# FFN outputs of the long sequence: accumulating DMA writes to DRAM in place of VectorE's additions in the plain groups

## The chip, the cores and the metric

The kernel runs on one NeuronCore of a Trainium2 chip as a single program. The metric is the device time of one execution in microseconds (us). Three runs of the kernel before took 3214.97, 3220.68 and 3206.7 us; their median, 3214.97 us, is the time before.

The engines are named as the profile names them: PE (TensorE matmuls; PEld is its weight load), DVE (VectorE), ACT (ScalarE), POOL (GpSimd) and SP (SyncE). DMA transfers are issued from two queues: SP's, which loads weights and inputs, and GpSimd's, which moves intermediate data to and from DRAM and is the one used for transfers that add into their destination.

## The reference

One encoder layer runs over two sequences, a sample of 1024 tokens ("s") and a prompt of 512 ("p"), D_MODEL = 1024:

```python
mod = (silu(c) @ w_ada + b_ada)                       # nine vectors of 1024 for each sequence
hn = rmsnorm(x, ffn1_norm) * (1 + sc1) + sh1
x = x + 0.5 * g1 * ((silu(hn @ w_gate) * (hn @ w_up)) @ w_down)     # FFN1, D_FF = 2816
hn = rmsnorm(x, mix_norm) * (1 + sc2) + sh2
proj = hn @ w_in                                       # q, k, v and three hyena inputs
x = x + g2 * (concat(rmsnorm(attention), rmsnorm(hyena)) @ w_out)
hn = rmsnorm(x, ffn2_norm) * (1 + sc3) + sh3
x = x + 0.5 * g3 * ((silu(hn @ w_gate) * (hn @ w_up)) @ w_down)     # FFN2
y = rmsnorm(x, final_norm)
```

The hyena branch convolves with long filters that come from a small network of the position; the filters do not depend on x, so they can be computed at any time before the mixer.

## The kernel before

Activations lie transposed, [feature, token], in 128 x 512 slices: eight slices (`KT`) for each chunk of 512 tokens, two chunks c for s and one for p. A product in fp32 is made of three matmuls on parts in fp32r: high weights by high activations, low by high, high by low. The parts of a weight (`hl<-raw`) are made by ACT and DVE, those of an activation (`act<-a`) too.

**The FFN of s** (`ffn`, L526) runs in 11 groups of two blocks of 128 hidden features. In a group, gate and up products go into PSUM tiles `gu`, ACT applies silu (`s<-gu`), DVE multiplies (`a<-s,gu`), and the parts `act` are made. Then `down` (L540) makes the group's share of the output: for each chunk eight slices dt, each of six matmuls of 512 columns into one of the two PSUM buffers of tile `dn`. That share, times the gain `Gc_s` of the layer's modulation, must be added to the residual x, which lies in SBUF as `q.xT` (tiles `xTs` in FFN1, `xRs` in FFN2; prompt: `xTp`, `xRp`).

A number `change` (7 in FFN1, 4 in FFN2) splits the groups in two sorts. Groups 0 to change-1 are plain. The later ones run in `ffn_fast` (L739), which saves matmuls by a scheme of seven products and needs more SBUF: the blocks in which x lies. The handover is in the last plain group, at L573 to L576: `spill_x` (L510) copies x to DRAM (`xscr_s`) by sixteen DMAs of 256 KB on GpSimd's queue, the side work is drained (below), and `Fast` takes x's blocks. In the plain groups before that, DVE adds each slice to x in SBUF, one instruction for each:

```python
stt(xv, ps, q.Gc[:, k, dt:dt + 1], xv, ALU.mult, ALU.add)
```

In the last plain group and in those of `ffn_fast`, `gather` (L520) does it instead: ACT scales the PSUM slice into an SBUF tile y (`pp`), and GpSimd issues a DMA that adds y to x in DRAM:

```python
se.activation(y, ps, AF.Copy, scale=q.Gc[:, k, dt:dt + 1])
nc.gpsimd.dma_start(q.xscr[c][dt], y, accum_op=ALU.add)
```

In the last group `reload_x` brings x back (tile `xRs<-xscr_s`).

**The order of the work.** A list scheduler sets each engine's order at build time; the chip keeps it. What it is given comes from `merge` (L1465), which interleaves the FFN with side work at a pace set by PLAN: the side work's progress follows that of the main work, measured in estimated engine time, against a total `mt`, 548e3 in stage A and 400e3 in stage E. ACT's and DVE's instructions of side work get a lower priority (LAG).

Stage A is FFN1 of s. Its side work is the filters of s, then a part of the modulation vectors (`ada_rest`: 1 MB loads into two buffers, `wada6a` and `wada6b`, on SP's queue, read by matmuls `mx<-wada6a,cs`), then the filters of p. For each of its eight steps a filter loads a small weight (`r<-in_hy_wo`, GpSimd's queue), splits it on ACT (`mscA<-r`) and DVE, makes the filter on PE and DVE, sums its absolute values on DVE (`r<-fT6b`), sums over channels on PE (`mx<-r,ones`), transforms it on PE and writes it to DRAM (`kscr_s`, `kscr_p`, GpSimd's queue). For p the transformed filter lies in tile `fT6b`, which the next step writes again.

Stage E is the hyena's end, the output projection and FFN2 of s. Its side work is p's mixer: attention, hyena, output projection (x of p is loaded from DRAM in halves, `xh6b<-xscr_p`, and written back), and the norm before FFN2 of p, whose parts go to DRAM (`nscr_p`).

At the start of the program the two chunks of x (`xin<-in_x_s`) are loaded, transposed on PE and copied to `xTs`, the modulation weights are loaded and multiplied, and the first FFN weights follow, all on SP's queue.

Of the kernel before, what the change touches and what calls it, by code (L numbers as in the profile page):

```python
# [11 lines left out]
F32 = mybir.dt.float32  # L12
# [5 lines left out]
P = 128  # L18
D = 1024
KT = D // P  # L20
# [72 lines left out]
def build(ctx, tc, nc, A):  # L93
# [34 lines left out]
    def mm(out, lhsT, rhs, start, stop, resume=False):  # L128
        work["pe"] += size(rhs) * (0.42 if rhs.dtype == F32R else 1.68)
        nc.tensor.matmul(out, lhsT, rhs, start=start, stop=stop, skip_group_check=resume)  # L130
# [5 lines left out]
    def tt(out, a, b, op):  # L136
        work["dve"] += 62.0 + 1.05 * size(out)
        ve.tensor_tensor(out, a, b, op=op)

    def stt(out, a, s, b, op0, op1):  # L140
        work["dve"] += 62.0 + 1.17 * size(out)
        ve.scalar_tensor_tensor(out, a, s, b, op0=op0, op1=op1)
# [8 lines left out]
    def dma(out, in_):  # L151
        nc.sync.dma_start(out, in_)

    def dmb(out, in_):
        MB.dma_start(out, in_)  # L155
# [4 lines left out]
    def gu():  # L160
        return pp.tile([P, 512], F32, tag="gu", bufs=3, name="gu")
# [9 lines left out]
    def t_s(shape=(P, 512), dt=F32):  # L171
        return fp.tile(list(shape), dt, tag="s", bufs=2, name="s")

    def t_a(shape=(P, 512), dt=F32):
        return fp.tile(list(shape), dt, tag="a", bufs=2, name="a")
# [4 lines left out]
    def t_act(shape=(P, 1024), dt=F32):  # L180
        return fp.tile(list(shape), dt, tag="act", bufs=4, name="act")

    def t_raw():
        return wp.tile([P, 1024], F32, tag="raw", bufs=3, name="raw")

    def t_hl():
        return wp.tile([P, 2, 512], F32R, tag="hl", bufs=6, name="hl")
# [13 lines left out]
    for qn, L in SEQ_LEN.items():  # L201
        q = Seq()
# [147 lines left out]
    def load_unit(src, dims):  # L350
        raw = t_raw()
        rv = raw if len(dims) == 0 else raw.rearrange("p (a b) -> p a b", b=dims[-1])
        dma(rv, src)
        hs = []
        for h in range(2):
            hl = t_hl()
            rh = raw[:, h * 512:(h + 1) * 512]
            se.activation(hl[:, 0], rh, AF.Copy)
            tt(hl[:, 1], rh, hl[:, 0].bitcast(F32), ALU.subtract)
            hs.append(hl)  # L360
        return hs

    def col_unit(w, c0):

        hs = load_unit(w[:, c0:c0 + P].rearrange("(kt p) c -> p kt c", p=P), (KT, P))
        return [[hs[kt // 4][:, i, (kt % 4) * P:(kt % 4 + 1) * P] for kt in range(KT)] for i in range(2)]

    def gemm_cols(ps, wv, xh, xl):
        gemm_along([ps], [wv], xh, xl)

    def gemm_along(pss, wvs, xh, xl, kts=range(KT)):

        for kt in kts:
            for ps, wv in zip(pss, wvs):
                mm(ps, wv[0][kt], xh[kt], kt == 0, False)
                mm(ps, wv[1][kt], xh[kt], False, False)
                mm(ps, wv[0][kt], xl[kt], False, kt == KT - 1)
# [132 lines left out]
    def spill_x(q):  # L510
        for c in range(q.C):
            for k in range(KT):
                dmb(q.xscr[c][k], q.xT[c][:, k])
# [6 lines left out]
    def gather(q, k, c, dt, ps, y):  # L520

        se.activation(y, ps, AF.Copy, scale=q.Gc[:, k, dt:dt + 1])
        nc.gpsimd.dma_start(q.xscr[c][dt], y, accum_op=ALU.add)  # L523


    def ffn(q, hn, wg, wu, wd, k, after, gate=None, last=None, get_dn=None,  # L526
            begin=None, change=None, late_loads=None):

        F = 2
        NG = NF // F

        passes = [(g, range(q.C)) for g in range(NG - 1)] + [(NG - 1, (c,)) for c in range(q.C)]
        if change is not None:
            passes = passes[:change]
        fast = None

        def down(g, cs_, acts):  # L540
            wds = [load_unit(wd[(g * F + f) * P:(g * F + f + 1) * P, :], ()) for f in range(F)]
            for c in cs_:
                sq = SumSq()
                for dt in range(KT):
                    ps = (get_dn or dn)()
                    for f in range(F):
                        wh, wl = (wds[f][dt // 4][:, i, (dt % 4) * P:(dt % 4 + 1) * P] for i in range(2))
                        act = acts[f, c]
                        mm(ps, wh, act[:, 0:512], f == 0, False)
                        mm(ps, wh, act[:, 512:1024], False, False)  # L550
                        mm(ps, wl, act[:, 0:512], False, f == F - 1)
                    if fast is not None:
                        gather(q, k, c, dt, ps, fast.pp[:, dt])
                        continue
                    xv = q.xT[c][:, dt]
                    stt(xv, ps, q.Gc[:, k, dt:dt + 1], xv, ALU.mult, ALU.add)
                    if g == NG - 1:
                        if last is not None:
                            last.add(c, dt)
                        else:  # L560
                            sq.add(xv)
                    if dt == 3 and q.C == 1:
                        yield
                if g == NG - 1:
                    if last is not None:
                        last.done(c)
                    else:
                        after(c, sq)
                yield
        late = None  # L570
        for n, (g, cs_) in enumerate(passes):
            acts = {}
            if change is not None and g == change - 1:  # L573
                spill_x(q)
                yield "drain"
                fast = Fast(hn)  # L576
            for f in range(F):
                f0 = (g * F + f) * P
                early = begin if g == 0 and f == 0 else None
                if early is not None:  # L580
                    sums = early()
                else:
                    wgv = col_unit(wg, f0)
                    wuv = col_unit(wu, f0)
                for c in cs_:
                    if early is not None:
                        G, U = sums[c]
                    elif g == 0 and f == 0:
                        G, U = gu(), gu()
                        gemm_along((G, U), (wgv, wuv), *hn[c])  # L590
                    else:
                        G, U = gu(), gu()
                        gemm_cols(G, wgv, *hn[c])
                        if g == 0 and gate is not None:
                            gate(False)
                        if q.C == 1 or change is not None:
                            yield
                        gemm_cols(U, wuv, *hn[c])
                    s = t_s()
                    se.activation(s, G, AF.Silu)  # L600
                    a = t_a()
                    tt(a, s, U, ALU.mult)
                    act = t_act((P, 1024), F32R)
                    se.activation(act[:, 0:512], a, AF.Copy)
                    tt(act[:, 512:1024], a, act[:, 0:512].bitcast(F32), ALU.subtract)
                    acts[f, c] = act
                    if fast is not None:
                        fast.make(f * q.C + c)
                    if g == 0 and gate is not None:
                        gate(f * q.C + c == F * q.C - 1)  # L610
                    yield

                if late is not None and (f == F - 1 or n < len(passes) - 1):
                    yield from late
                    late = None
            late = down(g, cs_, acts)
            if q.C > 1 or n == len(passes) - 1:
                yield from late
                late = None
        if change is not None:  # L620
            yield from ffn_fast(q, fast, wg, wu, wd, k, after, last, change, late_loads)
# [843 lines left out]
    def merge(name, main, *sides):  # L1465
# [3 lines left out]

        mt = PLAN[name][0]  # L1470
        m = 0.0
        todo = [[g, st, lead, f1, 0.0, 0.0] for g, (st, lead, f1) in zip(sides, PLAN[name][1:])]

# [51 lines left out]
    ring = [0]  # L1525
# [252 lines left out]
    def dn_or_mx():  # L1778
# [5 lines left out]


LAG = 300
PLAN = {"A": (548e3, (440e3, 0.0, 0.93)), "B": (77e3, (90e3, 0.0, 0.9)), "C": (952e3, (453e3, 0.0, 0.94)),
        "E": (400e3, (260e3, 0.0, 0.96))}
HOLD = {"A": 5e3, "B": 1.0, "C": 1.0, "E": 1.0}


# [39 lines left out]
```

## Time and profile before

| what | before |
|---|---|
| median of three runs | 3214.97 us |
| profiled execution | 3220.38 us |
| its span, first to last instruction | 3218.5 us |
| PE busy | 3126.8 us (97%) |
| DVE busy | 2007.2 us (62%) |
| ACT busy | 1282.6 us (40%) |
| POOL busy (issuing DMAs) | 466.6 us (14%) |
| mean granted TensorE clock | 0.988 |

The trace is of one execution, 5.4 us above the median of the runs. Stage A's plain groups run from about 100 to 625 us, the groups of `ffn_fast` to about 900 us; in stage E the plain groups lie between 2060 and 2420 us, those of `ffn_fast` up to about 2850 us. PEclk is the granted clock as a share of full speed: 1.00 is 2.4 GHz, 0.50 is 1.2 GHz. The DMA share is the mean busy share of the core's sixteen DMA engines.

### The profile page before, as it was taken

What the parts mean: (1) busy time and instruction counts of PE and PEld (TensorE: products, weight loads), DVE (VectorE), ACT (ScalarE), POOL (GpSimd) and SP (SyncE); (2) the same over time, 40 slices, a digit from 0 to 9 for tenths busy, and PEclk for the clock granted to TensorE, in tenths of its full rate; (3) what the DMA queues carried; (4) which work ended last, traced back from release to release, by engine and by line L of the source; (5) the groups of instructions that cost most, each with busy time, mean ns of one, the idle gap of its engine ahead of it and who ended that gap; (6) DMA issues with size and microseconds to landing.
All of it is one profiled execution on the core that took longest, in us unless ns stands there. A gap on an engine that the chain in (4) does not pass through costs nothing. (4 is left out here: it accounts for less than half of the span.)

```text
span 3218.5 us, 41377 instructions
## 1 busy us (share of the span) xinstructions
PE 3126.8 (97%) x15619; PEld 2551.2 (79%) x15619; DVE 2007.2 (62%) x3672; ACT 1282.6 (40%) x2296; POOL 466.6 (14%) x740
## 2 busy tenths in 40 slices
PE   7999999999998999999999999999999999999998
PEld 5788678888875889888777877788878888888887
DVE  5788366573471785987666467797474434464545
ACT  5211121255551432322656467414345554553233
POOL 1001201113211012001222101100122131300000
PEclk9999999999998999999999999999999999999999
DMA  7222632346646445534444344333466575753332
GB/s 263 88 80 89 218 111 76 127 99 129 143 178 225 137 140 159 193 125 141 128 128 148 121 145 123 123 89 96 129 168 120 120 131 119 180 180 99 98 96 75
DMA packets 328104, 429.18 MB, mean 133 GB/s; under 512 B 18640, under 2 KB 246120, under 8 KB 323200
## 3 DMA queue, kind: packets, MB, share of 16 engines
q0 software_dynamic: 70336, 200.01, 23.9%
q1 hardware_dynamic: 257536, 226.52, 22.9%
q8 instruction: 123, 2.02, 0.3%
q14 instruction: 77, 0.63, 0.1%
q10 hardware_dynamic: 32, 0.01, 0.0%
HBM read 316.62 MB, written 119.23 MB: 135 GB/s over the span
## 5 line engine op out<-in xcount | busy, mean ns | idle before, releaser
L130 PE MATMUL dn<-act,hl 128*128 128x512 f32 x2904 | 698.0, 394 | 13.1 <-DVE xRs L116 5.8
L116 DVE TENSOR_TENSOR hl<-raw,hl 128x512 fp32r<-128x512 f32 x612 | 418.7, 688 | 444.2 <-ACT hl L116 442.2
L116 ACT ACTIVATE hl<-raw 128x512 fp32r<-128x512 f32 x612 | 384.9, 631 | 730.0 <-PE gu L130 366.7
L130 PEld LDWEIGHTS dn<-act,hl 128*128 128x128 f32 x2904 | 541.9, 189 | 137.7 <-DVE xRs L116 9.6
L130 PE MATMUL gu<-hn1h,hl 128*128 128x512 f32 x1008 | 317.5, 394 | 0.0
L130 PE MATMUL gu<-hn3h,hl 128*128 128x512 f32 x736 | 231.6, 395 | 2.6 <-ACT hn3h L116 2.6
L130 PEld LDWEIGHTS gu<-hn1h,hl 128*128 128x128 f32 x1008 | 189.0, 189 | 48.2 <-issue 6.9
L130 PE MATMUL gu<-hn1ph,hl 128*128 128x512 f32 x704 | 225.0, 394 | 0.1
L130 PE MATMUL gu<-hn3ph,hl 128*128 128x512 f32 x704 | 217.2, 389 | 0.0
L130 PE MATMUL gu<-hn2h,hl 128*128 128x512 f32 x640 | 202.6, 397 | 3.3 <-DVE hl L116 1.9
L130 PE MATMUL gu<-hn1l,hl 128*128 128x512 f32 x504 | 198.2, 394 | 0.0
L523 POOL DMA_DIRECT2D xscr_s<-pp x140 | 119.3, 855 | 500.0 <-ACT pp L116 498.5
L130 PEld LDWEIGHTS gu<-hn3h,hl 128*128 128x128 f32 x736 | 138.2, 189 | 33.7 <-ACT hn3h L116 3.7
L130 PEld LDWEIGHTS gu<-hn3ph,hl 128*128 128x128 f32 x704 | 132.2, 188 | 27.3
L130 PEld LDWEIGHTS gu<-hn1ph,hl 128*128 128x128 f32 x704 | 130.9, 188 | 27.9 <-issue 2.6
L130 PE MATMUL gu<-hn3l,hl 128*128 128x512 f32 x368 | 144.2, 394 | 0.0
L130 PEld LDWEIGHTS gu<-hn2h,hl 128*128 128x128 f32 x640 | 119.3, 189 | 31.2 <-DVE hl L116 2.6
L130 PE MATMUL gu<-hn1pl,hl 128*128 128x512 f32 x352 | 138.3, 393 | 0.0
L130 PE MATMUL gu<-hn3pl,hl 128*128 128x512 f32 x352 | 137.0, 389 | 0.0
L116 DVE TENSOR_TENSOR a<-s,gu 128x512 f32<-128x512 f32 x87 | 59.5, 685 | 108.0 <-PE gu L130 100.3
L130 PE MATMUL gu<-hn2l,hl 128*128 128x512 f32 x320 | 125.5, 392 | 0.4 <-DVE hn2l L116 0.4
L116 ACT ACTIVATE pp<-dn,Gc_s 128x512 f32<-128x512 f32 x140 | 96.5, 689 | 70.2 <-PE dn L130 67.3
(454 smaller groups left out, 5697.1 us busy)
## 6 DMA issues: line engine op xcount, KB each, us to landing
raw<-in_ffn_w_gate SPq DMA_DIRECT2D x88, 512.0 KB, 3.9
raw<-in_ffn_w_up SPq DMA_DIRECT2D x77, 512.0 KB, 4.0
xscr_s<-pp POOLq DMA_DIRECT2D x140, 256.0 KB, 5.7
raw<-in_ffn_w_down SPq DMA_DIRECT2D x66, 512.0 KB, 3.6
raw<-in_w_in SPq DMA_DIRECT2D x48, 512.0 KB, 4.0
raw<-in_w_ada SPq DMA_DIRECT2D x31, 512.0 KB, 5.5
xRs<-xscr_s POOLq DMA_DIRECT2D x48, 256.0 KB, 5.1
raw<-in_w_out SPq DMA_DIRECT2D x24, 512.0 KB, 4.0
```

The lines of the kernel that those rows point to most:

```text
L116: return fn(*a, **k)
L130: nc.tensor.matmul(out, lhsT, rhs, start=start, stop=stop, skip_group_check=resume)
L523: nc.gpsimd.dma_start(q.xscr[c][dt], y, accum_op=ALU.add)
```

## The change

The residual x of s goes to DRAM at the first `down` of group 0, not in the last plain group, and the tiles that the plain groups' slices are scaled into (`yr`, one for each chunk) take the blocks in which x lay. All plain groups then add through `gather`. Two totals of PLAN are lowered (548e3 to 490e3, 400e3 to 380e3). All other code stands as it was.

```diff
@@ ffn
-        fast = None
+        fast, ring = None, []

         def down(g, cs_, acts):
+            if change is not None and not ring:
+                spill_x(q)
+                ring.extend(blk(c, [P, KT, 512], F32, "yr") for c in range(q.C))
             wds = [load_unit(...) for f in range(F)]
...
-                    if fast is not None:
-                        gather(q, k, c, dt, ps, fast.pp[:, dt])
+                    if change is not None:
+                        gather(q, k, c, dt, ps, ring[c][:, dt] if fast is None else fast.pp[:, dt])
                         continue
                     xv = q.xT[c][:, dt]
                     stt(xv, ps, q.Gc[:, k, dt:dt + 1], xv, ALU.mult, ALU.add)
...
             if change is not None and g == change - 1:
-                spill_x(q)
                 yield "drain"
                 fast = Fast(hn)
...
-PLAN = {"A": (548e3, ...), ..., "E": (400e3, ...)}
+PLAN = {"A": (490e3, ...), ..., "E": (380e3, ...)}
```

In the program 144 instructions `xTs<-dn` and `xRs<-dn` go from DVE (96 in stage A, 48 in stage E), 144 activations `yr<-dn` come to ACT, and 144 accumulating DMAs `xscr_s<-yr` to GpSimd's queue. The number of copies `xscr_s<-xTs` and `xscr_s<-xRs` stays at 32, and PE's instructions are the same in number.

On GpSimd's queue at the start of the program (`xTs_177` is chunk 0 of x, `xTs_341` chunk 1; `mlp_w`, `r` and `fT6b` belong to the filters), before:

```order
22 L155 DMA mscB<-in_decay_s 128x1024
23 L155 DMA mlp_w<-mlp_w 64x196
24 L155 DMA r<-in_hy_wo 64x2x128 x2
25 L155 DMA r<-in_hy_skip 128x128
26 L155 DMA r<-in_hy_wo 64x2x128 x2
27 L155 DMA r<-in_hy_skip 128x128
28 L155 DMA fT6b<-in_zt_s 17x1024
```

and in the changed kernel:

```order
22 L155 DMA mscB<-in_decay_s 128x1024
23 L155 DMA xscr_s<-xTs_177 128x512
24 L155 DMA mlp_w<-mlp_w 64x196
25 L155 DMA xscr_s<-xTs_177 128x512 x7
26 L155 DMA xscr_s<-xTs_341 128x512 x4
27 L155 DMA r<-in_hy_wo 64x2x128 x2
28 L155 DMA r<-in_hy_skip 128x128
29 L155 DMA xscr_s<-xTs_341 128x512 x4
30 L155 DMA r<-in_hy_wo 64x2x128 x2
31 L155 DMA r<-in_hy_skip 128x128
```

The sixteen copies of x, which stood after all filter work (rows 98 and 99), now stand among the first loads.

On the same queue beside the filters of p, in the last third of stage A's plain groups, before:

```order
83 L155 DMA kscr_p<-fT6b 128x1024
84 L155 DMA r<-in_hy_wo 64x2x128 x2
85 L155 DMA r<-in_hy_skip 128x128
86 L155 DMA mscB<-in_decay_p 128x512
87 L155 DMA kscr_p<-fT6b 128x1024
88 L155 DMA r<-in_hy_wo 64x2x128 x2
89 L155 DMA r<-in_hy_skip 128x128
```

and in the changed kernel (`yr_953` and `yr_954` are the tiles of the two chunks):

```order
101 L155 DMA mscB<-in_decay_p 128x512
102 L523 DMA xscr_s<-yr_953 128x512 x3
103 L155 DMA kscr_p<-fT6b 128x1024
104 L523 DMA xscr_s<-yr_953 128x512 x3
105 L155 DMA r<-in_hy_wo 64x2x128 x2
106 L155 DMA r<-in_hy_skip 128x128
107 L523 DMA xscr_s<-yr_954 128x512 x4
108 L155 DMA kscr_p<-fT6b 128x1024
109 L523 DMA xscr_s<-yr_954 128x512 x2
110 L155 DMA r<-in_hy_wo 64x2x128
111 L523 DMA xscr_s<-yr_954 128x512
112 L155 DMA r<-in_hy_wo 64x2x128
```

The filters' loads and writes now stand between the accumulating DMAs of one group's sixteen slices.

On ACT in the same group of the changed kernel:

```order
191 L116 ACTIVATE yr_953<-dn,Gc_s 128x512 x3
192 L118 ACTIVATE mscA<-r 128x256
193 L116 ACTIVATE yr_953<-dn,Gc_s 128x512
194 L118 COPY fA6a<-mx 128x256 x2
195 L116 ACTIVATE yr_953<-dn,Gc_s 128x512 x4
196 L116 ACTIVATE yr_954<-dn,Gc_s 128x512 x3
197 L118 ACTIVATE mscA<-r 128x256
```

The reads of PSUM tile `dn`, which stood on DVE, now stand on ACT's in-order queue, here with the filter's split of `r` and its copies of `mx` between them. In five places of the stage a split `mscA<-r` stands between two such reads.

## Rows read from the trace of the kernel before

**Rows 1.** The page: busy time per engine (part 1), then the GpSimd queue (part 3).

```profile
PE 3126.8 (97%) x15619; PEld 2551.2 (79%) x15619; DVE 2007.2 (62%) x3672; ACT 1282.6 (40%) x2296; POOL 466.6 (14%) x740
...
q0 software_dynamic: 70336, 200.01, 23.9%
```

**Rows 2.** Who evacuates dn, whole run: duration ns min/median/max, first and last start.

```profile
L116 ACT ACTIVATE pp<-dn,Gc_s x140: 670/690/695, 666.9 to 2769.4; 128x512 f32<-128x512 f32 x140
...
L116 DVE SCALAR_TENSOR_TENSOR xTs<-dn,Gc_s,xTs x96: 731/750/752, 106.3 to 622.8; 128x512 f32<-128x512 f32 x96
```

**Rows 3.** GpSimd's DMA issues on xscr_s, whole run, same columns as Rows 2.

```profile
L523 POOL DMA_DIRECT2D xscr_s<-pp x140: 837/852/1192, 667.9 to 2770.4; - x140
...
L155 POOL DMA_DIRECT2D xscr_s<-xTs x16: 542/542/547, 602.5 to 623.9; - x16
```

**Rows 4.** PE's waits, 110 to 650 us: total us, times, longest.

```profile
PE mx L130 <- DVE r L118: 15.6, 16, 1.6
PE dn L130 <- DVE xTs L116: 3.5, 2, 2.0
PE mx L130 <- DMA wada6b<-in_w_ada: 1.9, 1, 1.9
```

**Rows 5.** PE's waits, 2060 to 2420 us, same columns.

```profile
PE dn L130 <- DVE xRs L116: 5.1, 2, 2.7
```

**Rows 6.** Stretches: us; busy PE, PEld, DVE, ACT, POOL (count); clock, DMA share, GB/s.

```profile
20.00:30.00 10.00, 3.30 (x39) 1.50 (x32) 7.14 (x17) 2.93 (x5) 1.77 (x3) 0.79 1.03 308
100.00:300.00 200.00, 190.14 (x1121) 164.14 (x1120) 163.44 (x281) 33.56 (x58) 15.68 (x27) 1.00 0.26 77
330.00:375.00 45.00, 42.38 (x192) 28.69 (x191) 17.08 (x26) 4.39 (x7) 14.72 (x25) 0.96 0.87 303
500.30:507.10 6.80, 5.95 (x28) 5.79 (x28) 4.25 (x9) 0.37 (x1) 0.00 (x0) 0.50 0.27 77
640.00:840.00 200.00, 200.00 (x882) 165.15 (x881) 112.69 (x175) 102.62 (x169) 41.12 (x48) 1.00 0.57 116
2152.40:2155.80 3.40, 3.40 (x10) 2.63 (x9) 3.04 (x7) 1.16 (x2) 0.00 (x0) 0.50 0.44 145
2336.70:2340.10 3.40, 3.40 (x10) 2.66 (x9) 2.66 (x5) 0.00 (x0) 1.61 (x4) 0.50 0.49 166
```

**Rows 7.** In order of time: PE at 29 us, PE and DVE near 496 us: start, us.

```profile
29.42 1.94 PE L134 MATMUL dn<-ident,xin 128*128 128x128 f32 x8 [4.82 <-DMA xin<-in_x_s]
...
493.92 2.88 PE L130 MATMUL dn<-act,hl 128*128 128x512 f32 x12
498.81 1.68 PE L130 MATMUL dn<-act,hl 128*128 128x512 f32 x6 [2.01 <-DVE xTs L116]
501.35 0.77 PE L130 MATMUL mx<-r,ones 128*128 128x128 f32 x2 [0.85 <-DVE r L118]
...
496.02 1.29 DVE L118 TENSOR_TENSOR fT6b<-mx,mscB 128x512 f32<-128x512 f32 x2 [3.26 <-DMA kscr_p<-fT6b]
```

**Rows 8.** DMA, 650 to 900 us: queue share of 16 engines; issues, us to landing.

```profile
q0 software_dynamic: 10496, 20.98, 46.6%
...
xscr_s<-pp POOLq DMA_DIRECT2D x52, 256.0 KB, 5.7
xRs<-xscr_s POOLq DMA_DIRECT2D x16, 256.0 KB, 5.1
...
xscr_s<-s POOLq DMA_DIRECT2D x6, 256.0 KB, 6.0
```

**Rows 9.** The same view, 602 to 626 us: the sixteen copies of x.

```profile
q0 software_dynamic: 1258, 4.17, 46.0%
```

**Rows 10.** ACT's, then DVE's waits, 100 to 625 us, columns as in Rows 4.

```profile
ACT mscA L118 <- DMA r<-in_hy_wo: 19.6, 7, 9.0
...
DVE fT6b L118 <- DMA kscr_p<-fT6b: 8.8, 5, 4.5
```

**Rows 11.** Tile xh6b, 2060 to 2420 us: how long its DMAs take.

```profile
DMA to landing us min/median/max: 2.6/3.1/7.5
```

More of the change, by code (lines that the diff above doesn't have):

```diff
@@ L1786 @@
 LAG = 300
-PLAN = {"A": (548e3, (440e3, 0.0, 0.93)), "B": (77e3, (90e3, 0.0, 0.9)), "C": (952e3, (453e3, 0.0, 0.94)),
-        "E": (400e3, (260e3, 0.0, 0.96))}
+PLAN = {"A": (490e3, (440e3, 0.0, 0.93)), "B": (77e3, (90e3, 0.0, 0.9)), "C": (952e3, (453e3, 0.0, 0.94)),
+        "E": (380e3, (260e3, 0.0, 0.96))}
 HOLD = {"A": 5e3, "B": 1.0, "C": 1.0, "E": 1.0}
```

## The prediction

> **What bounds the kernel now.** I read the page's busy times first, then PE's waits in the two stretches that the change touches, then the same stretches beside a fast one by the table of windows, and last the DMA view. PE is busy for 97% of the span, DVE for 62%, ACT for 40%, POOL for 14% [rows 1]. So time can only come from what PE loses, and the reader should look there, not at the engines that are relieved. PE's waits are small in stage A's plain groups: 15.6 us in 16 pieces for the filter's sums, 3.5 us in two for DVE's reading of `dn`, 1.9 us for a modulation weight [rows 4]. In stage E it waits 5.1 us in two pieces for DVE's reading of `dn` [rows 5]. The waits for `dn` have an after-effect: behind each stands a stretch at half clock (granted clock 0.50, that is 1.2 GHz: 6.8 us after the wait at 498.81, 3.4 us after each of E's two) [rows 6, 7]. The pace is full in the fast groups, where the `gather` form runs already: PE is busy for 200.00 of 200 us with the DMA engines at 0.57 [rows 6].
>
> **What is removed and added.** DVE loses 144 additions of 0.75 us, 108 us [rows 2]; ACT gains 144 scalings of 0.69 us, 99 us [rows 2]; POOL gains 144 issues of 0.852 us, 123 us [rows 3]. Between 100 and 300 us DVE is busy 163 of 200 us and ACT 34 [rows 6], so both have the room and none becomes the bound by load. On PE these amounts cost nothing by themselves. What PE may gain or lose comes in seven terms.
>
> 1. *Stage A, DVE's reading of `dn`.* At 496 us PE waits 2.01 us because DVE, in order, had itself waited 3.26 us for the write of `kscr_p`; with the reading on ACT that cannot recur in this form. At most the two waits (3.5 us) and half of the 6.8 us at half clock (3.4 us) come back: 0 to -7, I take -5, since a wait for the filter's sum of 0.85 us stands right behind and keeps part of the clock's loss [rows 4, 6, 7].
> 2. *Stage E, the same.* 5.1 us and half of two stretches of 3.4 us: 0 to -8.5, I take -6 [rows 5, 6].
> 3. *Start-up.* The sixteen copies of x move from after the filters to the first tens of us. There the DMA engines are full (share 1.03 from 20 to 30 us) and PE waits 4.82 us for the second chunk of x [rows 6, 7]. In their old place the copies took 46.0% of 24 us, 11.0 us of all sixteen engines, 0.69 us each [rows 9]. Chunk 0's eight, 5.5 us, become ready while chunk 1 of x and the weights are still loading; chunk 1's eight come when PE has work. Between 0 and +11; I take +5.5. Their old place gives nothing back: PE is fully busy where the fast groups' loads and these copies meet. The Trainium skill ("DMA: Bandwidth & Descriptors", section "Issuing engines are not separate DMA queues") says that transfers from all issuing engines run on the same 16 DMA engines and interleave. By that rule GpSimd's queue is no cover for the copies and this term stands as priced; were the queue apart, it would be 0. No row of the kernel before shows the two together at start-up.
> 4. *Modulation weights in stage A.* From 330 to 375 us their loads keep the DMA engines at 0.87, and PE loses 2.6 us there [rows 6]. In the changed order these matmuls lie inside one group's `down`, whose sixteen gathers come at the same time. A gather costs: 46.6% of 250 us is 116.5 us of all engines for 64 gathers (52 from `pp`, 6 and 6 from `s` and `a`) and 16 reloads, 1.46 us each [rows 8]. Sixteen are 23 us; the free share of the 45 us is 6 us; 17 us are over. These can spread into the neighbouring stretch at 0.26 [rows 6]: 0 to +17, I take +4, nearer to the low end since the loads are issued ahead and PE has other groups' matmuls between.
> 5. *Filters of p behind gathers.* Three steps' `kscr_p` writes and `r` loads now stand among the gathers of one group, on a queue that is in order. DVE waits already 8.8 us in five for `kscr_p` [rows 10], and each gather ahead adds 1.46 us. Two ahead of each of three: 9 us more for DVE, of which PE sees a part: 0 to +12, I take +3.
> 6. *ACT's order.* ACT waits 19.6 us in seven for `r`, longest 9.0 [rows 10]. Before, nobody on PE stood behind it; now five splits stand between readings of `dn`. PE makes a slice in six matmuls of 200/882 = 0.227 us, 1.36 us [rows 6]; two buffers cover 2.7 us. The mean wait, 2.8 us, is just covered; the longest leaves 6.3. Twice the longest and some clock: 0 to +15, I take +3, nearer to the mean's row.
> 7. *Stage E's other loads.* The halves of p's x (`xh6b`) land in 3.1 us, at worst 7.5 [rows 11]; now they stand behind up to four gathers each, 5.8 us. Eight second-half loads at one such delay are covered by two buffers of `mx` and by other matmuls in part: 0 to +12, I take +2.5.
>
> The 15.6 us for the filter's sums I leave where they are, though DVE has less before them: the reduction itself stands between product and sum in both orders, with about as many matmuls in between. At best half of it, -8, comes back; at worst 0. I take 0.
>
> The sum: -5 - 6 + 5.5 + 4 + 3 + 3 + 2.5 = +7 us on the profiled execution of 3220.4 us, which is 5.4 us above the median of the runs [the table of times]. On the median: 3215 + 7 = 3222 us.
>
> The Trainium skill prices a GpSimd transfer otherwise ("DMA: Bandwidth & Descriptors", section "Anatomy of one DMA — SWDGE (gpsimd) path"): about 2.0 us plus bytes over 436e3, for 256 KB an estimate of 2.6 us to landing, 0.6 us of it for the bytes. The trace has 5.7 us to landing and 1.46 us of all engines for a transfer that adds into DRAM [rows 8], so the measurement decides; by the page's figure terms 4, 5 and 7 would shrink to some 40%, +4 in place of +9.5, and the time would be about 3216.
>
> **Rivals.**
>
> *DVE's relief wins.* All of terms 1 and 2 (-15.5) and half of the filter's sums (-8) come back, the copies at start-up cost a few us (+5), and the new waits are covered. 3215 - 15.5 - 8 + 5 is about 3197 to 3205, say 3200. For it: the fast groups run with gathers at full pace [rows 6]. Against it: there no side work shares the queue, and the loads that PE waits for are SP's alone.
>
> *The in-order GpSimd queue becomes the bound, slower.* Its place is the groups whose `down` meets side transfers: eight modulation loads, five `r`, three `kscr_p`, eight `xh6b`, 24 in all. Each is delayed by up to four gathers, landing time over pace (5.7/1.36), 5.8 us; the buffers cover 2.7. If one in three has no other work over it, 8 x 3.1 = 25 us, with a short stretch at half clock behind some (1.7 us each, five of them, 8 us) [rows 6, 8]. It decides from the point where a transfer is later than those 2.7 us while PE's next instruction needs it. With the start-up's 5.5 and the relief of 5: 3215 + 25 + 8 + 5.5 - 5, about 3248. For it: DMA at 0.87 beside the modulation loads [rows 6] and waits that exist already [rows 10]. Against it: PE's order has other matmuls in between nearly everywhere.
>
> *Nothing moves.* PE stays the bound, the start-up hides the copies behind transfers not needed soon, and relief and new waits cancel: 3215.
>
> **How the numbers follow.** The forecast, 3222 us (its own range 3208 to 3236), has a chance of 0.45; the relief, 3200, 0.2; the queue, 3248, 0.2; nothing, 3215, 0.15. A measurement of this kernel tells changes of more than 0.5%, 16 us, from none: faster is below 3199, slower above 3231. Faster: half of the relief, 0.10, and a remainder of 0.02: 0.12. Slower: nine tenths of the queue, 0.18, and a quarter of the forecast, 0.11: 0.29. The same: 0.59. The range leaves out one tenth at each end: 3197, where the relief's lower part begins, to 3252.
>
> **What would show it.** In the changed profile: term 1 and 2, no wait of PE for DVE on `dn` and full clock at their places; a wait `dn<-ACT yr` in their place would show term 6, with `mscA<-DMA r` ahead of it on ACT. Term 3: PE's wait for `xin` near 25 us grows from 4.8 to about 10 us, and the first FFN matmul comes 5 us later. Term 4: waits for `wada6a` and `wada6b` above the 1.9 us of before. Terms 5 and 7: longer landings of `kscr_p`, `r` and `xh6b`, and waits of PE behind them. The prediction is wrong if the plain groups of A and E lose less than before in sum by more than 16 us, or if one of the transfers named stalls PE for tens of us.

## The result and the profile after

The changed kernel takes 3252.58 us (median of four runs, 3251.6 to 3255.12); the kernel before takes 3215.19 us in the same comparison. The ratio is 1.0118 with a 95% interval of 1.0102 to 1.0134: 38 us slower (33 to 43). The forecast was 3222 us with a range up to 3252, so the time lies just outside it, and next to the 3248 us of the rival in which GpSimd's queue becomes the bound.

The page of the changed kernel, part 1, the GpSimd queue and the new issues (the last number is the median of the us to landing):

```profile
PE 3130.2 (96%) x15619; PEld 2557.0 (79%) x15619; DVE 1910.7 (59%) x3528; ACT 1372.7 (42%) x2436; POOL 593.3 (18%) x884
...
q0 software_dynamic: 91072, 237.77, 30.6%
...
xscr_s<-yr POOLq DMA_DIRECT2D x144, 256.0 KB, 7.2
```

DVE lost 97 us of busy time, ACT gained 90, POOL 127, about as counted, and PE's own work is as before [rows 1]. The loss is all in PE's idle time and clock. A `yr` transfer lands in 7.2 us, where a `pp` transfer took 5.7 [rows 8].

Where PE stands at landmarks of its own order (start times, us; the first matmul of its kind unless the row says last):

| landmark on PE | before | after | later by |
|---|---|---|---|
| first matmul of FFN1 of s (`gu<-hn1h`) | 41.5 | 44.7 | 3.2 |
| first of `ffn_fast` in stage A (`mx<-hn1h`) | 690.2 | 703.7 | 13.5 |
| last scores of stage C (`mx<-kTs`) | 1790.8 | 1810.2 | 19.4 |
| first matmul of FFN2 of s (`gu<-hn3h`) | 2057.9 | 2085.1 | 27.2 |
| first of `ffn_fast` in stage E (`mx<-hn3h`) | 2418.2 | 2450.3 | 32.1 |
| first transposition of the end (`dn<-ident,xRp`) | 3208.6 | 3240.9 | 32.3 |

The start-up, stage A's plain groups and stage E up to the handover hold 26 of the 32 us; `ffn_fast` adds nothing. Stage C's 6 us stand in an order of instructions that is the same in both kernels on PE, DVE and ACT; they are a matter of the execution, since a_548 and pace_a below come through the same stage with 1 us more and 1 us less. The profiled execution of before is 5.4 us above its median, which is why 32 us here stand for 38.

PE's waits in stage A's plain groups (total us, times, longest), which answer to [rows 4]:

```profile
PE mx L130 <- DVE r L118: 18.6, 15, 4.0
PE mx L130 <- DVE fA6a L118: 3.7, 1, 3.7
PE dn L130 <- ACT hl L116: 2.3, 1, 2.3
PE gu L130 <- ACT hl L116: 2.1, 1, 2.1
PE dn L130 <- ACT yr L116: 1.3, 1, 1.3
PE mx L130 <- DMA raw<-in_w_ada: 1.1, 1, 1.1
```

The waits of `dn` for DVE are gone, as forecast, and so are those for `wada6a` and `wada6b`. In their place PE waits 3.7 us for the filter of s (`fA6a`), 4.4 us for split weights (`hl`), and the longest wait for a filter's sum is 4.0 in place of 1.6 us.

The same in stage E, from the output projection to the handover; the answer to [rows 5]:

```profile
PE dn L130 <- DVE r L116: 3.4, 1, 3.4
PE gu L130 <- ACT hn3h L116: 2.0, 1, 2.0
...
PE dn L130 <- ACT pp L116: 4.5, 1, 4.5
PE dn L130 <- ACT yr L116: 3.8, 2, 2.5
```

Again no wait of `dn` for `xRs`, but 3.4 us for the norm's sums (`r`), 4.5 us for `pp` and 3.8 us for `yr`.

Engines by stretch, columns as in [rows 6]:

```profile
20.00:30.00 10.00, 2.13 (x28) 0.52 (x18) 4.07 (x13) 0.00 (x0) 2.15 (x5) 0.76 1.04 374
100.00:300.00 200.00, 189.16 (x1112) 163.29 (x1111) 148.50 (x263) 56.04 (x92) 45.23 (x62) 0.99 0.52 118
414.80:418.20 3.40, 3.40 (x18) 2.11 (x22) 1.12 (x2) 0.32 (x1) 0.00 (x0) 0.57 0.65 210
554.20:557.60 3.40, 3.05 (x14) 3.08 (x15) 1.00 (x4) 0.53 (x2) 0.00 (x0) 0.51 0.83 270
```

From 100 to 300 us the DMA share rose from 0.26 to 0.52; PE lost 10.8 us there, 9.9 before. The two short stretches are at half clock behind two of the new waits (granted 0.57 and 0.51, near 1.2 GHz).

The start-up on PE in order of time, to be held against the first line of [rows 7]:

```profile
33.27 6.15 PE L134 MATMUL dn<-ident,xin 128*128 128x128 f32 x28 [8.79 <-DMA xin<-in_x_s]
```

The wait for the second chunk of x grew from 4.82 to 8.79 us. This is term 3, near its size; with the same copies at start-up the wait is 6.8 us in a_only and 5.2 us in a_548 (both below).

At 412 to 423 us PE waits twice for `hl`. ACT, which makes it, waits for the FFN's weights on SP's queue; the second time:

```profile
422.72 1.15 ACT L116 ACTIVATE hl<-raw 128x512 fp32r<-128x512 f32 x2 [7.61 <-DMA raw<-in_ffn_w_gate]
```

What happened near 550 us, in order of time on POOL, DVE and PE:

```profile
542.52 0.86 POOL L523 DMA_DIRECT2D xscr_s<-yr  x1 [7.41 <-ACT yr L116]
543.11 0.82 POOL L155 DMA_DIRECT2D kscr_p<-fT6b  x1
543.88 0.93 POOL L523 DMA_DIRECT2D xscr_s<-yr  x1
...
549.94 1.29 DVE L118 TENSOR_TENSOR fT6b<-mx,mscB 128x512 f32<-128x512 f32 x2 [6.48 <-DMA kscr_p<-fT6b]
...
552.55 1.86 DVE L118 TENSOR_REDUCE r<-fT6b 128x128 f32<-128x1024 f32 x1
...
554.55 0.77 PE L130 MATMUL mx<-r,ones 128*128 128x128 f32 x2 [3.99 <-DVE r L118]
```

The write of `kscr_p` goes out at 543.1 us among the gathers; DVE, which will overwrite its source, waits 6.48 us for it; the filter's sum comes late, and PE waits 3.99 us. This is the mechanism of term 5 and of the second rival, step by step. The gathers are not its only source: pace_a, below, has waits of this kind without a gather in these groups.

In stage E, DMAs issued between 1960 and 2000 us (count, KB, us to landing), and then ACT and PE in order of time:

```profile
raw<-in_w_out SPq DMA_DIRECT2D x5, 512.0 KB, 11.4
...
xscr_s<-xRs POOLq DMA_DIRECT2D x5, 256.0 KB, 8.0
```

```profile
1992.36 0.63 ACT L116 ACTIVATE hl<-raw 128x512 fp32r<-128x512 f32 x1 [4.88 <-DMA raw<-in_w_out]
...
2002.08 1.84 PE L130 MATMUL dn<-ones,r 128*128 128x1 f32 x8 [3.44 <-DVE r L116]
```

The copies of x now stand beside the reload of x, and the weights of the output projection take 11.4 us (median of five) in place of the 5.5 us at the same step before. ACT waits for one of them, DVE's sums of squares are late, and PE waits 3.44 us. Of the two kernels below that change only stage E, e_only has this wait of PE (3.3 us), and e_gather_400, with the copies but the old pace, does not.

### The profile page after: what moved, and what is told of

Read it like the earlier page. It is cut to its first block, busy times and chain, and to the rows that moved or that the text cites. A ratio compares the mean times of both kernels' runs of the same rounds, so it can differ in the third digit from the quotient of the medians.

```text
span 3250.8 us, 41706 instructions
## 1 busy us (share of the span) xinstructions
PE 3130.2 (96%) x15619; PEld 2557.0 (79%) x15619; DVE 1910.7 (59%) x3528; ACT 1372.7 (42%) x2436; POOL 593.3 (18%) x884
## 4 chain that ended last, share of the span: by engine, by line
PE 75%; issue 8%; DMA 8%; DVE 5%; POOL 2%; ACT 2%; SPq 0%; POOLq 0%; DVEq 0%; ACTq 0%
PE gu L130 41%; PE dn L130 16%; PE mx L130 16%; DMA xscr_s<-yr 2%; PE mx L134 1%; POOL xscr_s L523 1%; DVE r L118 1%; PE dn L134 1%; DMA gscr<-rpb 1%; DMA r<-in_hy_wo 1%; DVE fT6b L118 1%; DMA xin<-in_x_s 1%; DMA raw<-in_w_ada 1%; DVE hl L116 0%; DMA mscA<-qscr_s 0%
## 5 line engine op out<-in xcount | busy, mean ns | idle before, releaser
L523 POOL DMA_DIRECT2D xscr_s<-yr x144 | 126.6, 998 | 214.4 <-ACT yr L116 196.0
L116 ACT ACTIVATE yr<-dn,Gc_s 128x512 f32<-128x512 f32 x144 | 98.9, 689 | 89.9 <-PE dn L130 87.6
```

Source lines behind the costliest of these rows:

```text
L116: return fn(*a, **k)
```

## The experiments

Sixteen kernels were run, each against the kernel before on the same chip. The ratios are to the kernel before, with 95% intervals; differences in us are the ratio's part of 3215 us.

**First: which stage, and the paces or the gathers?** `a_only` makes the change in FFN1 alone, with stage A's pace; `e_only` in FFN2 alone, with stage E's.

```diff
-            if change is not None and not ring:
+            if change == 7 and not ring:        # a_only; e_only: change == 4
...
-                    if change is not None:
+                    if change == 7 or fast is not None:
...
```

> Only FFN1 (stage A) has the change, with A's new pace of 490e3; FFN2 and the pace of E are those of before. Theory Q (transfers that stand behind the accumulating DMAs, on GpSimd's queue and on the DMA engines, come late and PE waits for them): the first matmul of ffn_fast in stage A comes 13 us later than before, as in the changed kernel (4.7 us of it in the start-up), and stage E is as before: 3228 to 3234 us. Theory P (the new paces order the work worse, not the transfers): the same as what old_plan loses. Theory N (what moved in stage C, whose order is unchanged, is a matter of the single execution): stage C's +6 us need not show.

> Only FFN2 (stage E) has the change, with E's new pace of 380e3; FFN1 is that of before. Theory Q: stage A as before, PE's late weights at x's copies (11.4 us to landing) and its waits behind xh6b stay, +13 us: 3226 to 3233 us. If E's loss came from a shift handed on by stage A, it would be gone here: 3213 to 3219.

Measured: a_only 3241.53 us, 1.0085 (1.0069 to 1.0102), +27 us; e_only 3225.79 us, 1.0034 (1.0023 to 1.0044), +11 us. The two add up to the whole 38. Stage A is the larger part and larger than expected; stage E's time is just under its expected range.

`plan_only` is the kernel before with the two new totals of PLAN; `old_plan` is the changed kernel with the old ones.

```diff
-PLAN = {"A": (548e3, ...), ..., "E": (400e3, ...)}
+PLAN = {"A": (490e3, ...), ..., "E": (380e3, ...)}      # plan_only; old_plan the reverse
```

> The kernel before with the two new paces (490e3, 380e3) alone; the additions stay on DVE. Theory Q: the paces cost little, 3210 to 3222 us. Theory P: most of the loss shows here, 3235 to 3250.

> The changed kernel with the old paces (548e3, 400e3). Theory Q: still slower by 25 to 45 us, 3240 to 3260. Theory P: back to 3215 to 3225.

Measured: plan_only 3227.79 us, 1.0045 (1.0030 to 1.0060), +14 us; old_plan 3233.49 us, 1.0060 (1.0045 to 1.0075), +19 us. Both times lie between the two theories, and neither holds alone: the paces cost 14 us without a gather in the plain groups, the gathers 19 us without the paces.

**Second: what in stage A's gathers costs?** All four start from a_only. A new edit makes the list scheduler order the engines anew, so it matters how much else moved. `a_plain_write` leaves the order as it is and makes the transfer a plain write (the sums are left out).

```diff
-        nc.gpsimd.dma_start(q.xscr[c][dt], y, accum_op=ALU.add)
+        dmb(q.xscr[c][dt], y)                    # in stage A's plain groups
```

> The kernel a_only (3241.5 us), where the DMAs of stage A's plain groups write the slice to DRAM without adding it (the sums are left out). The order on every engine and the number of GpSimd's issues are the same; only what a transfer costs falls, from 1.46 us of all DMA engines to about the 0.69 us of a copy. Theory Q, by the load on the DMA engines: most of stage A's loss beyond the start-up (some 15 us) goes, 3222 to 3230 us. If it is the queue's order or ACT's order and not the length of the transfers: 3236 to 3243.

Measured: 3227.87 us, 1.0041 (1.0027 to 1.0054). In the traces the order on DVE, ACT, POOL and SP is the same as in a_only through stage A's plain groups, so 14 of the 27 us go with the transfer's kind alone: its time to landing (median 6.5 us in a_only, 2.8 here) and what POOL spends on issuing it. First a_only, then a_plain_write, from 110 to 690 us:

```profile
DVE fT6b L118 <- DMA kscr_p<-fT6b: 21.9, 7, 7.5
...
PE mx L130 <- DVE r L118: 19.1, 15, 5.0
PE mx L130 <- DVE fA6a L118: 3.5, 1, 3.5
```

```profile
DVE fT6b L118 <- DMA kscr_p<-fT6b: 18.5, 7, 5.6
...
PE mx L130 <- DVE r L118: 15.6, 15, 3.1
```

The wait for `fA6a` is gone, and the longest waits for the write and for the filter's sum are shorter. What is left, +13 us, is about the start-up (group 0's first `s<-gu` on ACT starts at 68.2 us before, 74.9 in a_only, 74.5 here) and the pace of stage A (+6, pace_a below); that these two are all of it is an estimate.

`a_dve_scale` gives the scaling to DVE.

```diff
-        se.activation(y, ps, AF.Copy, scale=q.Gc[:, k, dt:dt + 1])
+        ts(y, ps, q.Gc[:, k, dt:dt + 1], ALU.mult)
```

> The kernel a_only, where DVE and not ACT scales the slice into yr in stage A's plain groups; the DMAs stay. Theory Q: the late transfers stay, 3235 to 3245 us. Theory S (ACT's in-order queue, where readings of dn stand behind hl and mscA, is what costs): back to 3220 to 3228.

Measured: 3244.34 us, 1.0096 (1.0078 to 1.0114), no better than a_only. So theory S finds no support. It is not excluded: with the scaling on DVE the scheduler also moved many other instructions (some 460 of 3260 matmuls in stage A's plain groups), and new waits can hide a gain. PE's waits in this kernel's stage A (columns as above) still show `hl`, now with one long wait, and `dn` waits for DVE:

```profile
PE gu L130 <- ACT hl L116: 11.4, 1, 11.4
PE dn L130 <- DVE yr L116: 4.4, 4, 1.8
```

`a_side_sp` sends the filters' loads and writes by SP's queue.

```diff
-                dmb(q.kscr[cb, o], X)
+                dma(q.kscr[cb, o], X)            # and so for r<-in_hy_wo and r<-in_hy_skip
```

> The kernel a_only, where the filters' loads of r and their writes of kscr go by SP's queue and not by GpSimd's. Theory Q in the form of the in-order GpSimd queue: the waits behind kscr and r (3.5 and 5.0 us, with their stretches at half clock some 10 us) go, 3228 to 3234 us. Theory Q in the form of full DMA engines, whichever queue: little, 3236 to 3243; slower still if the weights on SP's queue now stand behind the filters' loads.

Measured: 3218.50 us, 1.0020 (1.0010 to 1.0030). 21 of the 27 us are gone, more than expected. DVE's wait for the write, and PE's wait for the filter's sum, to be held against the lines of a_only above:

```profile
DVE fT6b L118 <- DMA kscr_p<-fT6b: 13.5, 6, 3.4
...
PE mx L130 <- DVE r L118: 13.0, 15, 1.7
```

The longest waits fell from 7.5 to 3.4 us and from 5.0 to 1.7. Engines from 100 to 640 us in a_only, a_plain_write and a_side_sp, in this order (columns as in [rows 6]; the last but one is the DMA share):

```profile
100.00:640.00 540.00, 505.68 (x2740) 416.72 (x2739) 290.41 (x538) 153.98 (x259) 138.82 (x193) 0.98 0.59 146
```

```profile
100.00:640.00 540.00, 515.53 (x2785) 424.82 (x2784) 292.29 (x541) 157.43 (x264) 109.78 (x196) 0.98 0.45 151
```

```profile
100.00:640.00 540.00, 518.41 (x2819) 427.51 (x2818) 298.09 (x546) 159.27 (x267) 107.36 (x138) 0.99 0.60 150
```

The share of the DMA engines is 0.59 in a_only and 0.60 in a_side_sp: the load is the same, PE is busy for 12.7 us more. So full DMA engines are not what costs; the place behind or beside the gathers in GpSimd's queue is, as far as this kernel can show it. Two things limit that. About 5 of the 21 us are there before the first gather: group 0's first `s<-gu` starts at 69.5 us, in a_only at 74.9. And a few instructions changed places (in stage A's plain groups 14 of 354 on ACT, 19 of 667 on DVE, some 50 of 3260 on PE). In a_plain_write, where none did, the load falls to 0.45, POOL is busy for 109.8 in place of 138.8 us, and the transfers land sooner.

`a_from_1` lets group 0 add on DVE, so that x is copied after group 0.

```diff
-            if change == 7 and not ring:
+            if change == 7 and g > 0 and not ring:
...
-                    if change == 7 or fast is not None:
+                    if ring or fast is not None:
```

> The kernel a_only, where group 0 still adds on DVE and the accumulating DMAs begin with group 1, so that x is copied to DRAM after group 0. Theory Q: the start-up's 3 to 5 us and group 0's wait for fA6a (3.5 us and its stretch at half clock) go, 3228 to 3234 us; the rest of stage A's loss stays.

Measured: 3226.54 us, 1.0039 (1.0024 to 1.0054), 15 us less than a_only, a little more than expected: FFN1's first matmul comes at 40.8 us, not 44.7, and PE's wait for `fA6a` falls from 3.5 to 0.4 us. A wait of 5.3 us for a filter's sum stays. Group 0's first `s<-gu` starts at 67.5 us, 7.4 earlier than in a_only: half of the 15 us is the start-up. The rest is not taken apart, since the order of the later groups changed too.

**Third: controls and the best version.** `b_side_sp` is the kernel before with the filters on SP's queue. `e_gather_400` is e_only at the old pace. `side_sp_400` is the whole change with the filters on SP's queue and the old pace in stage E; `from_1_sp_400` adds a_from_1's edit to it.

> The kernel before, where the filters' loads of r and writes of kscr go by SP's queue; no other change. Theory Q (what cost was their place behind the accumulating DMAs): there are none in stage A's first six groups here, so no gain, 3208 to 3220 us, and a_side_sp's 23 us over a_only come from the pair. Rival: SP's queue is better for the filters in any case, and a_side_sp only hides the loss: 3190 to 3203.

> The kernel e_only (3225.8 us) with stage E's old pace of 400e3: FFN2 gathers in all groups, FFN1 as before. Theory P for stage E: the pace alone makes its loss, 3210 to 3218 us, DVE's waits on dn paid back by those on ACT. Theory Q for stage E: 3222 to 3228.

> The whole change with the filters' loads and writes on SP's queue and stage E's old pace. If the two causes are the whole loss, it stands with before: 3212 to 3222 us; if something else is left, 3228 or more.

> As side_sp_400, and in FFN1 group 0 still adds on DVE, so that x goes to DRAM after the start-up. Theory Q: 4 to 8 us less than side_sp_400, 3203 to 3214 us, at or below the kernel before.

Measured: b_side_sp 3210.28 us, 0.9991 (0.9977 to 1.0004); e_gather_400 3214.97 us, 1.0002 (0.9991 to 1.0013); side_sp_400 3221.04 us, 1.0024 (1.0013 to 1.0036); from_1_sp_400 3213.26 us, 0.9997 (0.9984 to 1.0010). SP's queue is no clear gain by itself (-3 us, interval -7 to +1), so most of a_side_sp's 21 us comes from moving the filters away from gathers and copies. This control runs at the old pace: a part of stage A's pace cost may be in the 21 us too, and no run separates it. Stage E's gathers cost nothing measurable at the old pace. With the filters moved and stage E's old pace 8 us are left (side_sp_400); only with the start-up relieved as well does the change come back to the time before, and no version with gathers beats it. In e_gather_400 PE waits in stage E for ACT in place of DVE:

```profile
PE dn L130 <- ACT pp L116: 4.5, 1, 4.5
PE gu L130 <- ACT hn3h L116: 2.6, 2, 2.0
PE gu L130 <- ACT s L116: 2.3, 1, 2.3
```

The 5.1 us of [rows 5] are gone and 6.8 us for `pp` and `s` have come.

**Fourth: what was still open.** `a_548` is a_only at the old pace; `pace_a` and `pace_e` are the kernel before with one new pace each; `a_kscr_sp` is a_side_sp with the loads of r left on GpSimd's queue.

> Stage A gathers in all groups at the old pace of 548e3, stage E as before. If the pace of stage A costs 8 us beside the gathers (old_plan 3233.5 against a_only 3241.5 us): 3231 to 3235. If it costs nothing and the difference was noise: 3238 to 3243.

> The kernel before with stage A's new pace of 490e3 alone. From plan_only's trace (3 us later at the end of stage A, where executions of one order differ by some 5): 3213 to 3219 us. If stage A's pace is part of plan_only's 13 us: 3220 or more.

> The kernel before with stage E's new pace of 380e3 alone. Theory P for stage E: all of e_only's 11 us, 3223 to 3229. If the pace costs only with the gathers: 3212 to 3217.

> The kernel a_only, where the filters' writes of kscr go by SP's queue and their loads of r stay on GpSimd's. If the writes, for which DVE waits, carry the loss: 3220 to 3228 us. If the loads of r do: 3234 to 3241.

Measured: a_548 3234.89 us, 1.0060 (1.0045 to 1.0075); pace_a 3221.52 us, 1.0020 (1.0010 to 1.0029); pace_e 3223.10 us, 1.0022 (1.0004 to 1.0040); a_kscr_sp 3262.47 us, 1.0148 (1.0131 to 1.0165).

| part | ratio to before | us |
|---|---|---|
| gathers in stage A, old pace (a_548) | 1.0060 | +19 |
| pace of stage A (pace_a) | 1.0020 | +6 |
| gathers in stage E, old pace (e_gather_400) | 1.0002 | +1 |
| pace of stage E (pace_e) | 1.0022 | +7 |
| sum | | +33 |
| the whole change | 1.0118 | +38 |

The parts are 33 us of the 38 (its interval begins at 33); in stage E pace and gathers together (e_only, +11) cost 3 us more than one by one, in stage A (a_only, +27) 2 us more, neither clear of the intervals. In pace_a two waits of the filters of p grow with no gather beside them, from 110 to 690 us (before, the longest were 4.5 [rows 10] and 1.6 us [rows 4]):

```profile
DVE fT6b L118 <- DMA kscr_p<-fT6b: 12.2, 5, 5.7
...
PE mx L130 <- DVE r L118: 18.0, 16, 4.9
```

So the new pace and the gathers of stage A lead to the same waits, each by itself (a_548, gathers at the old pace: up to 5.4 and 4.2 us). In pace_e the largest wait is one that before does not show, from 1920 to 2470 us:

```profile
PE mx L130 <- DVE hyP L118: 7.0, 1, 7.0
```

PE reaches p's hyena, the side work, before DVE has its operand: the lower total sends the side work ahead, and this step comes 7.0 us too early on PE. In the whole change and in e_only, at the same pace, this wait does not occur; there PE waits for `r`, `pp` and `yr` as shown above. How the 11 us of stage E divide is therefore open beyond the times in the table.

a_kscr_sp is a miss of both its expectations: 20 us slower than a_only. ACT's wait for r from 110 to 690 us and PE's for the filter's sum:

```profile
ACT mscA L118 <- DMA r<-in_hy_wo: 54.8, 13, 8.6
...
PE mx L130 <- DVE r L118: 31.9, 15, 6.3
```

With the writes moved, DVE waits less for them, but the loads of r, left on GpSimd's queue among the gathers, come later: ACT waits 54.8 us, 34.7 in a_only. So the writes alone don't carry the loss. The order of the loads between the gathers changed too in this kernel, and which of the two, order or queue, made it worse than a_only is open. It also shows that moving these transfers can cost as much as it gains.

## Why the prediction was wrong

- **The step that failed first: the two totals of PLAN had no term.** The working went through removed additions, gathers and copies, and took the new order as given. Alone, without a gather in the plain groups, the paces cost 14 us (plan_only), half of it in each stage. The sum of +7 could not have held them.
- **Terms 3 to 6 in stage A were mis-sized.** With term 1 they come to -5 + 5.5 + 4 + 3 + 3 = +10.5 us; a_548 measured +19. The start-up was right (wait for x 4.8 to 8.8 us; 4.6 us later at 104 us, up to 6.7 at group 0's first `s<-gu` in a_only). Term 5, the filters' transfers behind gathers, was 3 us in a range up to 12, and was taken for p's filters alone; a_plain_write shows that the length of the accumulating transfers is worth 14 us in an unchanged order, and a_side_sp that the filters' place beside gathers and copies is worth up to 21. It struck s's filters too (`fA6a`, 3.7 us), and behind the wait of 3.99 us stands a stretch at half clock (0.51), which I had left out of this term.
- **Term 4 named the right place and the wrong transfer.** PE does not wait for `wada6a` or `wada6b` in the changed kernel; the FFN's weights behind them on SP's queue come late, and ACT's split `hl` holds PE 4.4 us near 412 to 423 us. At the old pace (a_548) it is the other way round: 3.0 us for `wada6a`, none for `hl`. Its price of 1.46 us is a mean over 64 gathers and 16 plain reloads; with the 0.69 us of a copy for a reload, a gather alone comes to an estimated 1.65 us, which would not have moved the term much.
- **Term 6 hardly occurred.** PE waits 1.3 us for `yr` in stage A, and giving the scaling to DVE brings no time back (a_dve_scale, whose order differs).
- **Terms 1, 2 and 7: the waits went, the time did not come.** None of DVE's waits on `dn` is left, but in stage E new ones for ACT take their place: terms 2 and 7 were to give -6 + 2.5, e_gather_400 measured +1 us. Term 7 alone was not measured; the halves of p's x land in 4.4 us in place of 3.1 (median), and no wait of PE names them.
- **The filter's sums** gave nothing back, as forecast: 15.6 us before, 18.6 after. That they grew, the longest from 1.6 to 4.0 us, belongs to term 5 and to the pace.
- **The rivals.** The second, GpSimd's queue, named the mechanism that a_plain_write shows and a_side_sp bears out, and its 3248 us was near; its time was right partly by chance, since a third of the loss is the paces, and stage E's gathers, which it counted, cost nothing. The first was wrong: relieving an engine that is not the bound gave back only its own two short waits in each stage. I gave the queue 0.2 because PE's order has other matmuls in between; what I missed is that `ffn_fast` was no model for it, since there no side transfers share GpSimd's queue. The text had said this, as an argument against the first rival, and did not use it for the sum.

## What to carry to other kernels

Before an addition is turned into a DMA, list which other transfers stand on the same queue in that stretch and who waits for them; a stretch in which the same DMA runs freely says nothing if it has no such neighbours. A constant that steers a scheduler is an edit with a price of its own: give it a term, or at least a bound, even where every instruction stays. And an engine that is relieved gives back only those waits of the bound engine that it ends last; here 3.5 and 5.1 us.

## What was not expected of the hardware

Moving the filters' transfers from GpSimd's queue to SP's was worth 21 us at the same DMA share (0.59 and 0.60), some 5 us of it at start-up. The Trainium skill ("DMA: Bandwidth & Descriptors", section "Issuing engines are not separate DMA queues") says that issuing from several engines only saves the sequencer's time to initiate; here the landing changed too: the slowest `kscr_p` write took 7.8 us in a_only and 3.4 in a_side_sp, so the measurement decides, and the queue can matter more than that. The same page of the Trainium skill, section "Queues, rings and completion order", has each DMA engine take turns between the queues it has work for; the fall of DVE's longest wait for `kscr_p` from 7.5 to 3.4 us agrees with it. A 256 KB transfer that adds into DRAM landed in 6.5 us (median) in stage A's plain groups of a_only, a plain write of the same size, at the same places in the same order, in 2.8 us (a_plain_write).

Executions of one order of instructions differ by some us: in e_only, whose stage A is that of before, `ffn_fast` begins at 685.0 us, and 690.2 in before's trace. Single landmarks are read with that in mind, and only the timed comparisons settle 10 us.
